# Where the output weights of a decoder step are split into high and low parts: in the stage of the chunk rows, or beside the last group of products

## The chip, the cores and the metric

The kernel runs on one core of a Trainium2 chip. The metric is the device time of one execution in microseconds (us). A core has five engines, each with an in-order queue of its own: TensorE (PE) for matrix products, VectorE (DVE), ScalarE (ACT), GpSimd (POOL) and SyncE (SP), which here issues most of the DMA transfers. On-chip memory is SBUF; products are summed up in PSUM banks, from which DVE or ACT must evict them before the bank is used again. An engine waits for another by semaphores.

## What is computed

One step of a hybrid decoder layer over 1024 prompt rows and 8 × 8 sample rows (T = 1088 columns, as most tensors are held transposed), with model width D = 1024:

```
proj = h @ w_in                                  # one projection into all branches
P = (pool_mix(u_pool) * silu(z_pool)) @ w_pool_out
S = gated_rmsnorm(SSD(conv(xBC)) + D*x, z_ssm) @ w_ssm_out      # 2048 -> 1024
m = sigmoid(g_pool) * P + sigmoid(g_ssm) * S
x = x + gate * (m @ w_o)                         # w_o: 1024 x 1024
y = rmsnorm(x)
```

Products are made to fp32 precision out of a faster format, fp32r: a factor is split into a high part (a copy in fp32r) and a low part (the factor less its high part), and a product is three matmuls, high·high, high·low and low·high. So each weight has to be split once, by a copy on ACT and a subtraction on POOL or DVE, before PE can use it. This study is on the weight w_o, 4 MB, which is used only at the end.

## The kernel before, in words

The work goes through four stages.

1. **Projections** and convolution, to about 830 us. Beside them the weights w_pool_out and w_ssm_out are split (`splits`), and their halves are stored in DRAM (`wp_d`, `ws_d`).

2. **Chunk rows**, about 830 to 1130 us (L1783 to L1822). The SSD recurrence runs over 4 groups of 8 chunks, 32 steps of `seq`. For each chunk there are a load of decay terms (tile `dec` from DRAM `acs_d`, 512 KB), an exponential on ACT (L1498), DVE's L1520 and L1522, and PE's transposes and products (L1506, L1508, L1213, L1530); ACT also evicts L1511, L1513. Between them stand pieces of the dense products (`pieces`, matmuls at L359 to L361): P for all eight row blocks (`P_unit`) and S for groups 0 to 2 (`S_unit`, whose first group is evicted by ACT at L1739). PE's order of work in this stage is written down by the program (`in_line`), so PE stands wherever the next item isn't ready. From chunk 13 on, two calls per chunk go to the generator `wo_splits` (L1764 to L1781), which cuts w_o into 16 pieces of 128x512. For each piece there are a load on SP's queue into `pw` (L1771; two buffers), a copy to fp32r on ACT into `ph` (L1777; one buffer), a store of the high half from ACT's queue (L1778), a subtraction on POOL (L1779), and a store of the low half on SP's queue (L1773). The halves go to DRAM, `wo_d`.

3. **Tail**, about 1130 to 1200 us (L1829 to L1932). First the norm's scales: sums of squares (matmul, L1843), a square root on ACT (L1845), a reciprocal, eight diagonal matrices on DVE (L1851) and products that spread them (L1852) into three PSUM banks. Then come eight units, one for each block of 128 channels of m: the last group's product `S_unit(3, m)`, three blocks of 12 matmuls in three rotating PSUM banks. `m_done` (L1887 on) loads `R` from `gs_d` (the gate, 128x1088) and multiplies it by the scales on DVE (three L1891, which read PSUM), loads P's part from `m1_d`, and for each block evicts PSUM on DVE (L1898). Behind the last block stand a multiplication on DVE (L1903) and an addition on POOL (L1904), both 128x1088 with all operands in SBUF. `m_split` (L1868 on) splits the result: 64 sample columns (ACT L1871, DVE L1872) and 1024 prompt columns (ACT L1882, DVE L1883). `wo_prep(k)` loads both halves of row block k of w_o from `wo_d` (L1864, L1865; 512 KB each): blocks 0 to 3 into a tile that was freed by the earlier stage (`Y4(hp)`), block 4 into buffers of the tail, 5 to 7 only behind the last unit into tiles freed by it (`late`). `samples[k]` is the sample rows' product with block k (four matmuls, L1877). The order of instructions within an engine is set by the framework's scheduler, apart from the places where the program gives a priority or writes the order down. Weights for the products are loaded two units ahead (`ready`, L459 and L460).

4. **End**, about 1200 to 1296 us (L1978 to L2019): eight row tiles, each 8 × 3 matmuls for each half of the columns (L1995 to L1997) of m with w_o, then gate, residual and norm; a tile's output is stored while the next one is being made.

Of the kernel before, what the change touches and what calls it, by code (L numbers as in the profile page):

```python
# [8 lines left out]
F32 = mybir.dt.float32  # L9
F32R = mybir.dt.float32r  # L10
AF = mybir.ActivationFunctionType
ALU = mybir.AluOpType
# [8 lines left out]
P = 128  # L21
D = 1024
# [24 lines left out]
def tile_pool_ssd_step(  # L47
# [6 lines left out]
    nc = tc.nc  # L54
    uid = [0]

    def nm(s):
        uid[0] += 1
        return f"{s}_{uid[0]}"
# [10 lines left out]
    def open_(name, bufs, side="left"):  # L70
        cm = tc.tile_pool(name=name, bufs=bufs, side=side, reuse_waits="tile")
        kept.append(cm)
        return cm.__enter__()
# [36 lines left out]
    load = nc.sync.dma_start  # L110
    store_ = nc.scalar.dma_start
    mm = nc.tensor.matmul
    act = nc.scalar.activation
    V = nc.vector
# [224 lines left out]
    def in_line(engines, begin=False):  # L339
        traced = nc.cur_bb.bb.instructions  # L340
        for i in traced[len(traced) if begin else line[0]:]:
            if i.engine in engines:
                if i.engine in line[1]:
                    tc.add_manual_dep(i, line[1][i.engine], mybir.DependencyInfo(
                        mybir.DependencyClass.NoSync, mybir.DependencyReason.DATA), reason="in_line")
                line[1][i.engine] = i.name
        line[0] = len(traced)
# [42 lines left out]
    def dram(name, shape, dt=F32):  # L390
        return dr.tile(list(shape), dt, tag=name, name=name)
# [13 lines left out]
    def behind(engine, n=0):  # L405

        of = (i for i in reversed(nc.cur_bb.bb.instructions) if i.engine == engine)
        for _ in range(n):
            next(of)
        return tc.issue_after(next(of))  # L410
# [1070 lines left out]
    def sample_end(g):  # L1481
        sz = ckt([P, 4, P], "sz", 3)[:, :, :NS]
        load(sz, z_d[g][:, :, SEQ:])
        v = ckt([P, 4, P], "v")[:, :, :NS]
        load(v, ys_d[g])
        finish(g, SEQ, NS, v, sz)
# [219 lines left out]
    ck = right.__enter__()  # L1706
# [20 lines left out]
    def S_unit(g, m, done):  # L1727
        def run(w):
            rh = [yh[g][:, q] for q in range(4)]
            rl = [yl[g][:, q] for q in range(4)]  # L1730
            yield from gemm_(w, rh, rl, 4, done(m))
        return (ready(ws_d[g][m]), run)
# [22 lines left out]
    def pieces():  # L1755
        ws = first_ws
        nxt = len(ws)
        for i, (pf, run) in enumerate(prods):
            while nxt < len(prods) and nxt <= i + 1:
                ws[nxt] = prods[nxt][0]()  # L1760
                nxt += 1
            yield from run(ws.pop(i))
    pc_ = pieces()
    wo_d = [dram(f"wo{k}", [P, 2, D]) for k in range(8)]  # L1764

    def wo_splits():
        raws = {}
        for n in range(18):
            if n < 16:
                raws[n] = ck.tile([P, 512], F32, tag="pw", name=nm("pw"), bufs=2)  # L1770
                load(raws[n], w_o[0, n // 2 * P:n // 2 * P + P, n % 2 * 512:n % 2 * 512 + 512])  # L1771
            if n > 1:
                load(wo_d[(n - 2) // 2][:, 1, n % 2 * 512:n % 2 * 512 + 512], raws.pop(n - 2))  # L1773
            yield
            if n < 16:
                hi = ck.tile([P, 512], F32R, tag="ph", name=nm("ph"), bufs=1)
                act(hi, raws[n], AF.Copy)  # L1777
                store_(wo_d[n // 2][:, 0, n % 2 * 512:n % 2 * 512 + 512], hi.bitcast(F32))  # L1778
                nc.gpsimd.tensor_tensor(raws[n].bitcast(F32R), raws[n], hi.bitcast(F32), ALU.subtract)  # L1779
            yield  # L1780
    wos = wo_splits()  # L1781
    RATE = 2.56
    FRONT = 4  # L1783

    def products(t):

        nonlocal made
        while made < RATE * t:
            next(pc_, None)
            made += 1  # L1790
# [5 lines left out]
        next(pc_)  # L1796
    next(seq[0])
    for i in range(len(seq)):
        if i > 12:
            next(wos, None)  # L1800
        if i + 1 < len(seq):
            with behind(mybir.EngineType.DVE, 1 - i) if i < 2 else ExitStack():
                next(seq[i + 1])
        products(i + 0.4)
        if i > 0:
            next(seq[i - 1], None)
        if i > 12:
            next(wos, None)
        next(seq[i], None)
        if i % NC == 3:  # L1810
            sample_end(i // NC)
        if i + 3 < len(seq):
            next(seq[i + 3])
        if i + 2 < len(seq):
            with behind(mybir.EngineType.Activation) if i == 0 else ExitStack():
                next(seq[i + 2])
        products(i + 1.0)
    next(seq[-1], None)
    for it in (pc_, wos):
        for _ in it:  # L1820
            pass
    in_line((mybir.EngineType.PE,))  # L1822
    right.__exit__(None, None, None)
    while right_all:
# [3 lines left out]

    mp = ctx.enter_context(tc.tile_pool(name="mp", bufs=8, side="right", reuse_waits="tile"))  # L1829
    mq = open_("mq", 5)  # L1830

    def M(shape=(P, T), dt=F32):
        return mq.tile(list(shape), dt, tag="m", name=nm("m"))
# [7 lines left out]
    for c in range(9):  # L1841
        n = min(P, T - c * P)
# [5 lines left out]
    for c in range(9):  # L1848
        n = min(P, T - c * P)
# [4 lines left out]
    wo, mh, ml = [None] * 8, [None] * 8, [None] * 8  # L1854
    w4 = [Y4(hp), Y4(hp)]
    pso = [PB(), PC()]
    samples = []

    def wo_prep(k, mem):
        if k < 4:  # L1860
            hi, lo = w4[0][:, k, :D], w4[1][:, k, :D]
        else:
            hi, lo = mem((P, D), F32R), mem((P, D), F32R)
        load(hi.bitcast(F32), wo_d[k][:, 0])  # L1864
        load(lo.bitcast(F32), wo_d[k][:, 1])  # L1865
        wo[k] = (hi, lo)

    def m_split(k, mem):  # L1868

        sh = sm.tile([P, P], F32R, tag="stc", name=nm("sh"), bufs=4)  # L1870
        act(sh[:, 0:NS], acc[k][:, SEQ:], AF.Copy)  # L1871
        V.tensor_tensor(sh[:, NS:P], acc[k][:, SEQ:], sh[:, 0:NS].bitcast(F32), ALU.subtract)  # L1872

        def sample_mm():
            for part in wo[k]:
                for half in range(2):
                    mm(pso[half], sh, part[:, half * 512:half * 512 + 512],  # L1877
                       start=(k == 0 and part is wo[k][0]), stop=(k == 7 and part is wo[k][1]))
        samples.append(sample_mm)
        hi, lo = mem((P, SEQ), F32R), mem((P, SEQ), F32R)  # L1880
        for o, n in (((0, 384), (384, 384), (768, 256)) if k == 7 else ((0, SEQ),)):
            act(hi[:, o:o + n], acc[k][:, o:o + n], AF.Copy)  # L1882
            V.tensor_tensor(lo[:, o:o + n], acc[k][:, o:o + n], hi[:, o:o + n].bitcast(F32), ALU.subtract)  # L1883
        mh[k], ml[k] = hi, lo
# [22 lines left out]
    def tail_unit(m):  # L1907
        pf, run_ = S_unit(3, m, m_done)

        def run(w):  # L1910
            for _ in run_(w):
                pass
            if m < 5:
                wo_prep(m, M)
            if m < 7:
                m_split(m, M8 if m < 4 else G)
            if m < 5:
                with tc.high_priority(PRIO):
                    samples[m]()
        return (pf, run)  # L1920
    run_units([tail_unit(m) for m in range(8)])
    y4 = [Y4(hs), Y4(hs)]
# [4 lines left out]
    for k in (5, 6):  # L1927
        wo_prep(k, late)
        samples[k]()
    wo_prep(7, late)  # L1930
    m_split(7, late)
    sample_mm = samples[7]  # L1932
# [116 lines left out]
```

## Time and profile before

| what | value |
|---|---|
| median of three runs | 1296.04 us (1295.9, 1296.04, 1298.21) |
| the profiled execution's own time | 1297.28 us |
| its span on the core | 1295.4 us (1.88 us lie around it) |
| mean granted clock of PE | 0.996 |
| PE busy in the span | 1258.9 us, 97% |
| DVE, ACT, POOL busy | 893.3, 699.5, 671.9 us |
| moved by DMA | 251.68 MB, 194 GB/s in the mean |

How to read the rows of the profile. A row of a timeline is: start in us, length in us, engine, line of the program, operation, output tile <- input tiles, shape and type of output and inputs, and how many such instructions the row takes together (x3 is three behind each other). Brackets at the end tell how long the engine stood idle before it, and what ended the idle time: "[2.96 <-DMA pw<-in_w_o]" is 2.96 us, ended by the landing of the transfer from w_o into `pw`. Matmuls overlap in the records, so that successive starts, not lengths, give PE's pace. A queue's rows (SPq) are the issue of a transfer and not its duration. A row of groups gives the count of one kind of instruction, then smallest, median and largest duration in ns, and when the first and the last began.

### The profile page before, as it was taken

To read this page: it belongs to the slowest core of one execution; us is meant where nothing else is said; L and a number is where in the kernel's file an instruction comes from. 1 tells how busy PE (TensorE), PEld (TensorE's weight loads), DVE (VectorE), ACT (ScalarE), POOL (GpSimd) and SP (SyncE) were. 2 spreads that over 40 slices of the span, in tenths; PEclk is the share of its full clock that TensorE was granted. 3 is DMA by queue.
4 is the path that set the end of the run, shared out by engine and by line. 5 is a ranking of instruction groups with operands and counts; after the bars stand their busy time and mean duration, and the time that the engine had idled before them with its cause. 6 is when DMAs were issued, how large, how long until landed. Compare 5 with 4: busy or idle time off the path is not lost.

```text
span 1295.4 us, 26382 instructions
## 1 busy us (share of the span) xinstructions
PE 1258.9 (97%) x9739; PEld 1170.7 (90%) x9739; DVE 893.3 (69%) x1512; ACT 699.5 (54%) x1658; POOL 671.9 (52%) x563
## 2 busy tenths in 40 slices
PE   7999999999999999999999999999998999999998
PEld 6779999989999999999999999888897889999786
DVE  4686678966979688676766675577665877476433
ACT  4665347365656555555666543687886776201111
POOL 1007668677868777564445444266675656214000
PEclk9999999999999999999999999999999999999999
DMA  9736355465456544444566574999887665475631
GB/s 330 242 115 223 113 163 164 147 203 177 136 161 212 157 144 149 151 146 135 169 182 192 154 207 159 336 362 382 296 270 249 200 210 171 160 262 161 227 105 50
DMA packets 233793, 251.68 MB, mean 194 GB/s; under 512 B 31265, under 2 KB 177905, under 8 KB 233658
## 3 DMA queue, kind: packets, MB, share of 16 engines
q1 hardware_dynamic: 161568, 171.60, 41.6%
q10 hardware_dynamic: 72098, 78.41, 17.6%
q8 instruction: 77, 1.26, 0.4%
q14 instruction: 50, 0.41, 0.1%
HBM read 167.06 MB, written 83.01 MB: 193 GB/s over the span
## 4 chain that ended last, share of the span: by engine, by line
PE 73%; issue 8%; DMA 6%; POOL 4%; ACT 4%; DVE 4%; ACTq 0%; SPq 0%; POOLq 0%; DVEq 0%
PE mm L608 7%; PE ps L608 7%; PE ps L609 7%; PE ps L610 7%; PE mm L610 6%; PE mm L609 6%; PE mm L359 4%; PE mm L360 4%; PE mm L361 4%; PE ps L1213 2%; PE ps L1997 2%; PE ps L1995 2%; PE ps L1996 2%; PE pc L1530 2%; PE ps L1216 2%
## 5 line engine op out<-in xcount | busy, mean ns | idle before, releaser
L168 POOL TENSOR_TENSOR wlo<-rawA,whi 128x512 fp32r<-128x512 f32 x120 | 180.0, 1505 | 176.8 <-ACT whi L165 100.3
L168 POOL TENSOR_TENSOR wlo<-raw,whi 128x512 fp32r<-128x512 f32 x92 | 147.2, 1607 | 123.2 <-ACT whi L165 109.3
L359 PE MATMUL mm<-Y,whi 128*128 128x352 f32 (+1 forms) x480 | 164.2, 342 | 2.0 <-ACT G L1739 1.4
L360 PE MATMUL mm<-Y,whi 128*128 128x352 f32 (+1 forms) x480 | 158.1, 329 | 1.0 <-DVE Y L1566 1.0
L361 PE MATMUL mm<-Y,wlo 128*128 128x352 f32 (+1 forms) x480 | 157.5, 328 | 0.0
L608 PE MATMUL mm<-Y,whi 128*128 128x272 f32 x496 | 146.5, 295 | 0.7 <-DVE GA L624 0.5
L610 PE MATMUL mm<-Y,wlo 128*128 128x272 f32 x496 | 144.2, 291 | 2.9 <-POOL wlo L168 2.4
L608 PE MATMUL ps<-Y,whi 128*128 128x272 f32 x496 | 143.4, 289 | 2.3 <-ACT o L808 2.2
L609 PE MATMUL ps<-Y,whi 128*128 128x272 f32 x496 | 143.0, 288 | 0.0
L609 PE MATMUL mm<-Y,whi 128*128 128x272 f32 x496 | 142.6, 288 | 0.0
L610 PE MATMUL ps<-Y,wlo 128*128 128x272 f32 x496 | 142.6, 287 | 0.0
L1056 DVE SCALAR_TENSOR_TENSOR GA<-GA,cvT,GA 128x1112 f32<-128x1112 f32 x72 | 128.5, 1787 | 1.6 <-ACT GA L1053 1.5
L165 ACT ACTIVATE whi<-rawA 128x512 fp32r<-128x512 f32 x125 | 78.3, 627 | 88.8 <-PE ps L609 44.9
L165 ACT ACTIVATE whi<-raw 128x512 fp32r<-128x512 f32 x96 | 58.9, 627 | 105.7 <-DVE raw L554 51.3
L359 PEld LDWEIGHTS mm<-Y,whi 128*128 128x128 f32 x480 | 90.8, 189 | 8.8 <-issue 4.6
L610 PEld LDWEIGHTS mm<-Y,wlo 128*128 128x128 f32 x496 | 93.4, 188 | 4.7 <-POOL wlo L168 3.5
L608 PEld LDWEIGHTS mm<-Y,whi 128*128 128x128 f32 x496 | 93.3, 188 | 3.4 <-ACT whi L165 0.7
L608 PEld LDWEIGHTS ps<-Y,whi 128*128 128x128 f32 x496 | 93.3, 188 | 2.9 <-ACT o L808 2.4
L609 PEld LDWEIGHTS mm<-Y,whi 128*128 128x128 f32 x496 | 93.4, 188 | 0.9
L610 PEld LDWEIGHTS ps<-Y,wlo 128*128 128x128 f32 x496 | 93.4, 188 | 0.0
L609 PEld LDWEIGHTS ps<-Y,whi 128*128 128x128 f32 x496 | 93.3, 188 | 0.0
L360 PEld LDWEIGHTS mm<-Y,whi 128*128 128x128 f32 x480 | 90.8, 189 | 1.7 <-DVE Y L1566 1.6
(450 smaller groups left out, 3801.1 us busy)
## 6 DMA issues: line engine op xcount, KB each, us to landing
rawA<-in_w_in SPq DMA_DIRECT2D x46, 512.0 KB
dec<-acs_d SPq DMA_DIRECT2D x32, 512.0 KB
xbc<-GA ACTq DMA_DIRECT2D x24, 512.0 KB
xb<-xbc SPq DMA_DIRECT2D x32, 384.0 KB
rawA<-in_w_in SPq DMA_DIRECT2D x32, 256.0 KB
pw<-in_w_ssm_out ACTq DMA_DIRECT2D x32, 256.0 KB
ws<-ph ACTq DMA_DIRECT2D x32, 256.0 KB
ws<-pw SPq DMA_DIRECT2D x32, 256.0 KB
```

What stands on the lines that cost most here:

```text
L165: ins = act(hi[:, :, :ncols], raw[:, :, :ncols], AF.Copy)
L168: (eng or nc.gpsimd).tensor_tensor(lo[:, :, :ncols], raw[:, :, :ncols], hi[:, :, :ncols].bitcast(F32), ALU.subtract)
L359: mm(ps[:, :n], a, rh[k][:, o:o + n], start=(k == 0), stop=False)
L360: mm(ps[:, :n], a, rl[k][:, o:o + n], start=False, stop=False)
L361: mm(ps[:, :n], b, rh[k][:, o:o + n], start=False, stop=(k == nk - 1))
L608: mm(p, hi, ah, start=(k == 0), stop=False)
L609: mm(p, hi, al, start=False, stop=False)
L610: mm(p, lo, ah, start=False, stop=(k == 3))
L1056: V.scalar_tensor_tensor(d[:, :n], rp[:, k:k + n], cvT[:, 24 * k + mc:24 * k + mc + 1], d[:, :n], ALU.mult, ALU.add)
L1213: mm(o[hh], xd[:S, 2 * q + hh, :], dec[:S, 2 * q + hh], start=True, stop=state is None)
L1216: mm(o[hh], state[:, h * 64:h * 64 + 64], cE[:, h], start=False, stop=True)
L1530: mm(pu, bt, xw.rearrange("p h d -> p (h d)"), start=True, stop=True)
```

## The change

`wo_splits` and its calls in the chunk rows' loop go. The first five row blocks (`LATE = 5`) are loaded from w_o as they are in `wo_prep`, 512 KB each into a new pool `mr` (tag `wr`, two buffers), copied to fp32r by ACT and subtracted by POOL, and both parts stay on chip. The last three are split by a new function `wo_store`, called behind units 2, 3 and 4: load, ACT copy into `wh` (one buffer), store of the high half, subtraction on DVE, store of the low half, both stores issued by SP. Behind the last unit `wo_prep` loads them from DRAM as before. The sample rows' products follow one unit later than before (`samples[m - 1]`). Two lines fewer stand ahead of the tail's functions, so that line L1898 of before, for one, is L1894 of the changed kernel (L1903: L1899; L1904: L1900; L1872: L1868; L1883: L1879; L1995: L1993).

```diff
-    wo_d = [dram(f"wo{k}", [P, 2, D]) for k in range(8)]
-
-    def wo_splits():
-        raws = {}
-        for n in range(18):
-            if n < 16:
-                raws[n] = ck.tile([P, 512], F32, tag="pw", name=nm("pw"), bufs=2)
-                load(raws[n], w_o[0, n // 2 * P:n // 2 * P + P, n % 2 * 512:n % 2 * 512 + 512])
-            if n > 1:
-                load(wo_d[(n - 2) // 2][:, 1, n % 2 * 512:n % 2 * 512 + 512], raws.pop(n - 2))
-            yield
-            if n < 16:
-                hi = ck.tile([P, 512], F32R, tag="ph", name=nm("ph"), bufs=1)
-                act(hi, raws[n], AF.Copy)
-                store_(wo_d[n // 2][:, 0, n % 2 * 512:n % 2 * 512 + 512], hi.bitcast(F32))
-                nc.gpsimd.tensor_tensor(raws[n].bitcast(F32R), raws[n], hi.bitcast(F32), ALU.subtract)
-            yield
-    wos = wo_splits()
+
+    LATE = 5
+    wo_d = {k: dram(f"wo{k}", [P, 2, D]) for k in range(LATE, 8)}
...
     for i in range(len(seq)):
-        if i > 12:
-            next(wos, None)
         if i + 1 < len(seq):
...
-        if i > 12:
-            next(wos, None)
         next(seq[i], None)
...
     mq = open_("mq", 5)
+    mr = open_("mr", 2)
...
-        load(hi.bitcast(F32), wo_d[k][:, 0])
-        load(lo.bitcast(F32), wo_d[k][:, 1])
+        if k < LATE:
+            raw = mr.tile([P, D], F32, tag="wr", name=nm("wr"))
+            load(raw, w_o[0, k * P:k * P + P, :])
+            act(hi, raw, AF.Copy)
+            nc.gpsimd.tensor_tensor(lo, raw, hi.bitcast(F32), ALU.subtract)
+        else:
+            load(hi.bitcast(F32), wo_d[k][:, 0])
+            load(lo.bitcast(F32), wo_d[k][:, 1])
         wo[k] = (hi, lo)
+
+    def wo_store(k):
+        raw = mr.tile([P, D], F32, tag="wr", name=nm("wr"))
+        load(raw, w_o[0, k * P:k * P + P, :])
+        hi = mr.tile([P, D], F32R, tag="wh", name=nm("wh"), bufs=1)
+        act(hi, raw, AF.Copy)
+        load(wo_d[k][:, 0], hi.bitcast(F32))
+        V.tensor_tensor(raw.bitcast(F32R), raw, hi.bitcast(F32), ALU.subtract)
+        load(wo_d[k][:, 1], raw)
...
-            if m < 5:
+            if m < LATE:
                 wo_prep(m, M)
             if m < 7:
                 m_split(m, M8 if m < 4 else G)
-            if m < 5:
+            if 1 < m < 5:
+                wo_store(m + 3)
+            if 0 < m <= LATE:
                 with tc.high_priority(PRIO):
-                    samples[m]()
+                    samples[m - 1]()
```

(`load` issues a transfer on SP's queue, in either direction; `store_` one on ACT's.)

More of the change, by code (lines that the diff above doesn't have):

```diff
@@ L1818, in tile_pool_ssd_step @@
     next(seq[-1], None)
-    for it in (pc_, wos):
-        for _ in it:
-            pass
+    for _ in pc_:
+        pass
     in_line((mybir.EngineType.PE,))
```

## The prediction

> **What bounds the kernel now.** I read the page's busy shares first, then the windows by stage, then each engine's timeline where TensorE (PE) stood still.
>
> ```profile
> PE 1258.9 (97%) x9739; PEld 1170.7 (90%) x9739; DVE 893.3 (69%) x1512; ACT 699.5 (54%) x1658; POOL 671.9 (52%) x563
> ```
> ```profile
> 830.00:950.00 120.00, 118.37 (x950) 104.81 (x950) 87.16 (x116) 97.16 (x271) 79.50 (x87) 1.00 0.98 336
> 950.00:1005.00 55.00, 49.81 (x392) 44.05 (x389) 32.29 (x42) 37.68 (x102) 33.02 (x36) 1.00 0.80 254
> 1005.00:1130.00 125.00, 125.00 (x987) 112.57 (x987) 88.85 (x129) 76.91 (x213) 69.41 (x88) 1.00 0.58 185
> 1130.00:1145.00 15.00, 15.00 (x92) 14.97 (x90) 5.42 (x17) 0.41 (x2) 0.00 (x0) 0.89 0.71 248
> 1145.00:1200.00 55.00, 54.41 (x312) 51.45 (x311) 42.30 (x69) 8.97 (x15) 21.05 (x9) 1.00 0.57 192
> ```
>
> PE is 97% busy: only its idle time and its own work can move the end. The windows' columns are the length, the busy time (and instructions) of PE, PEld, DVE, ACT and POOL, then the granted clock, DMA share and GB/s. The splits of w_o run from 837.8 to 992.7 us; the chunk rows go on without them to 1130. With splits PE idles 120 − 118.37 = 1.63 and 55 − 49.81 = 5.19 us; without them, 0.00. In the tail (last group of products, 1130 to 1200) it idles 0.59.
>
> **The change part by part.**
>
> *Taken out of the chunk rows.* The 5.19 us are three waits of PE, 1.42 + 2.09 + 1.68:
>
> ```profile
> 975.61 0.63 ACT L1777 ACTIVATE ph<-pw 128x512 fp32r<-128x512 f32 x1 [2.96 <-DMA pw<-in_w_o]
> 978.37 0.44 ACT L1739 ACTIVATE G<-mm 128x352 f32<-128x352 f32 x1
> 991.97 0.63 ACT L1777 ACTIVATE ph<-pw 128x512 fp32r<-128x512 f32 x1 [4.82 <-DMA wo<-ph]
> 1003.60 1.06 ACT L1498 ACTIVATE cE<-dec 128x1024 f32<-128x1024 f32 x1 [3.34 <-DMA dec<-acs_d]
> ```
> ```profile
> 980.54 1.22 DVE L1520 TENSOR_TENSOR dec<-dec,ps 128x1024 f32<-128x1024 f32 x1 [7.26 <-POOL sz L1475]
> 1000.34 1.22 DVE L1520 TENSOR_TENSOR dec<-dec,ps 128x1024 f32<-128x1024 f32 x1 [6.18 <-ACT ps L1513]
> ```
> ```profile
> 978.86 0.43 PE L359 MATMUL mm<-Y,whi 128*128 128x352 f32 x1 [1.42 <-ACT G L1739]
> 983.15 0.63 PE L1506 MATMUL ps<-ident,xb 128*128 128x128 f32 x4 [2.09 <-DVE cE L1522]
> 1002.84 0.30 PE L1508 MATMUL ps<-ident,xb 128*128 128x128 f32 x1 [1.68 <-DVE cE L1522]
> ```
>
> ACT stood 2.96 us before the copy at 975.61, for its load, and 4.82 us before the one at 991.97, because `ph` has one buffer whose store had not landed. ACT works in order, so the eviction L1739 (978.37), then L1513, came late; DVE L1520 stood 7.26 and 6.18 us; PE came last. All three waits hang on ACT standing for a split. The stage also loses 16 copies, 16 subtractions, 48 transfers of 256 KB (12 MB; SP issues 32, ACT 16):
>
> ```profile
> L1777 ACT ACTIVATE ph<-pw x16: 612/619/632, 837.8 to 992.0; 128x512 fp32r<-128x512 f32 x16
> L1779 POOL TENSOR_TENSOR pw<-pw,ph x16: 1273/1296/1457, 839.0 to 992.7; 128x512 fp32r<-128x512 f32 x16
> ```
>
> That is 16 × 0.619 = 9.9 us of ACT, 16 × 1.296 = 20.7 of POOL, none itself on PE's path. Order of PE's instructions in the stage is unchanged. What would be late next is the load of `dec` (ACT's 3.34 us at 1003.60), in a stage with 12 MB less to move. Bounds: 0 (that load takes over) to 5.19 + 1.63 = 6.8. I take **−5.2**, as the 125 us without splits show no wait.
>
> *Put beside the last group.* Rows 0–4: a 512 KB load, an ACT copy, a POOL subtraction each. Rows 5–7: load, copy, store, DVE subtraction, store, and both halves loaded later. DMA falls from 12 + 8 MB to 10, but all in the tail and the stretch behind it; SP issues there go from 16 to 20. ACT gains eight copies of 128x1024 (1.04 each, row below), 8.3 us, and it is busy 0.41 of 15 and 8.97 of 55: hidden. DVE gains 3 × 1.21 (at 42.30 of 55); POOL 5 × 2.4 = 12 us (2.54 × 1024/1088, from L1904), on top of 21.05 of 55. Mean load is no bound; order is, and who blocks whom:
>
> ```profile
> 1151.40 1.29 DVE L1903 TENSOR_TENSOR G<-G,R 128x1088 f32<-128x1088 f32 x1
> 1153.61 2.85 DVE L1903 TENSOR_TENSOR G<-G,R 128x1088 f32<-128x1088 f32 x1
> 1156.85 2.30 DVE L1872 TENSOR_TENSOR sh<-G,sh 128x64 fp32r<-128x64 f32 x1
> 1160.84 1.21 DVE L1883 TENSOR_TENSOR m<-G,m 128x1024 fp32r<-128x1024 f32 x1
> 1161.97 0.22 DVE L1872 TENSOR_TENSOR sh<-G,sh 128x64 fp32r<-128x64 f32 x1
> ```
> ```profile
> 1152.77 2.54 POOL L1904 TENSOR_TENSOR G<-G,m 128x1088 f32<-128x1088 f32 x1 [34.67 <-DVE G L1903]
> 1156.54 2.53 POOL L1904 TENSOR_TENSOR G<-G,m 128x1088 f32<-128x1088 f32 x1 [1.23 <-DVE G L1903]
> ```
>
> The same L1903 takes 1.29 alone and 2.85 when it starts inside POOL's addition of 1152.77–1155.31; L1872 takes 0.22 alone and 2.30 inside 1156.54–1159.07, ending with it. So a DVE instruction with both inputs in SBUF and a POOL one shut each other out. Each new subtraction on POOL is therefore 2.4 us in which DVE's in-order queue can stand, with PE's evictions (L1898) behind it.
>
> The Trainium skill, "SBUF — State Buffer", section "🔬 SBUF: two separate sides", says that the two engines' shared port pair is an exclusive lock, kept for the whole instruction by whoever starts first. It speaks against this change, and the two rows above agree with it; by plain sharing of the bandwidth the tail's term below would be about 0.
>
> ```profile
> 1135.02 2.05 PE L1843 MATMUL ps<-ones,sq_acc 128*128 128x1 f32 x18
> ```
> ```profile
> 1155.51 1.04 ACT L1882 ACTIVATE m<-G 128x1024 fp32r<-128x1024 f32 x1
> ```
>
> The chain, in the times of before. The earliest POOL can start row 0 is about 1136 (the products of group 2 end where the sums of squares begin, 1135.0, with rows 0 and 1 taken to be loaded already; a copy of this shape takes 1.04); rows 0 and 1 end about 1141. Row 2's load takes the buffer freed at 1138.6. A 544 KB load took 1166.31 to 1169.99 = 3.7 us, so it lands about 1142.4 and is subtracted until 1145.8; row 3's load then follows and its subtraction runs about 1151.6–1154.0. There it meets the chain of L1903 and L1904. Alternating from there (multiply 1.29, addition 2.5): first multiply ends 1155.3, addition 1157.9, second pair 1161.8, DVE's subtraction of row 6 1162.9, POOL's row 4 until 1165.5, DVE's L1883 1166.6, the third multiply 1167.8 and the third addition 1170.4; before, the third multiply ended 1166.28.
>
> ```profile
> 1164.99 1.29 DVE L1903 TENSOR_TENSOR G<-G,R 128x1088 f32<-128x1088 f32 x1
> 1166.20 1.42 DVE L1898 TENSOR_TENSOR G<-mm,G 128x384 f32<-128x384 f32 x3
> 1169.99 1.42 DVE L1891 TENSOR_TENSOR R<-ps,R 128x512 f32<-128x512 f32 x3 [2.37 <-DMA R<-gs]
> ```
> ```profile
> 1145.51 0.32 SPq L459 DMA_DIRECT2D whi<-ws  x1
> ...
> 1166.31 0.32 SPq L1888 DMA_DIRECT2D R<-gs  x1
> ```
> ```profile
> 1166.80 0.44 PE L359 MATMUL mm<-Y,whi 128*128 128x384 f32 x1
> 1168.99 0.32 PE L359 MATMUL mm<-Y,whi 128*128 128x352 f32 x1
> 1174.40 0.44 PE L359 MATMUL mm<-Y,whi 128*128 128x384 f32 x1 [0.48 <-DVE G L1898]
> ```
>
> DVE's order changes at this place: before, the third multiply is followed by all three evictions of group 3 (1166.20, 1.42). After, behind the first eviction stand L1872 of the second unit (shut out until 1170.4), three L1891 (1.42) and L1883 (1.21); the other evictions end about 1173.5. PE's second block of the next product wants that bank and began at 1168.99: it starts about 1173.6, **+4.6**, from which before's wait of 0.48 at 1174.40 is taken, as it falls inside: **+4.1**. Bounds: 0 (the subtractions fall between evictions) to 6 (a second such meeting, 2.5 − 0.6).
>
> Other queues. SP now has stores behind ACT and DVE, and ahead of weight loads; the weights issued at 1145.51 are used at 1166.80, 21 us later, so a hold of some 4 us is covered, and if it were not, PE would stand for those 4 us once. The square root's table load and scales now stand behind two row copies:
>
> ```profile
> 1116.59 1.28 ACT L1845 ACT_TABLE_LOAD   x1 [0.46 <-ACT xD L1550]
> 1137.11 0.41 ACT L1845 ACTIVATE rs<-ps,eps 128x8 f32<-128x8 f32 x2 [19.23 <-PE ps L1843]
> 1142.83 1.05 PE L1852 MATMUL ps<-dg,ones 128*128 128x128 f32 x8
> ```
>
> The scales come about 1138.3 instead of 1137.1, and PE asks for them at 1142.83: cost 0, up to 1.3 + 1.04 if two more copies go ahead.
>
> *The end.* Before, two sample products wait for their rows:
>
> ```profile
> 1205.23 0.47 PE L1877 MATMUL ps<-Y,sh 128*128 128x512 f32 x1 [0.38 <-DMA Y<-wo]
> 1206.89 0.50 PE L1877 MATMUL ps<-Y,sh 128*128 128x512 f32 x1 [0.27 <-DMA Y<-wo]
> ```
>
> With samples one unit later, more of PE's work stands between these loads and their use: **−0.65**, between 0 and −0.65. Rows 5–7 are stored some 25 us before they are read.
>
> Sum: −5.2 + 4.1 − 0.65 = −1.75. The profiled execution has 1297.28 us (span 1295.4 and 1.88 around it), 1.24 above the median of 1296.04: 1295.5 in its terms, **1294.3** against the median.
>
> **The rivals.**
>
> *The meeting on DVE misses PE.* If row 3's load lands some 4 us sooner, or DVE's queue leaves evictions ahead of the shut-out L1872, POOL's subtractions fall in its idle time (34.67 us before 1152.77). For it: 21.05 of 55 busy. Against it: only two raw buffers, so row 3 waits for row 1. Tail 0 to 1.3: 1296.04 − 5.85 = 1290.2 to 1291.5.
>
> *Another wait takes the place of the splits' (slower).* ACT at L1498 waits for `dec`, whose load is on the chain of waits for
>
> ```profile
> 813.58 8.80 DMA dec<-acs_d
> ```
>
> 8.80 us at its longest there, and 3.34 at 1003.60, after the last split. If those loads hold PE at 978, 983 and 1002 as well, the stage gains under 0.8, and the tail's +4.1 decides: 1296.04 − 0.5 + 4.1 − 0.65 = 1299.0 (1298.6 to 1300.1). It decides from a gain below 0.8. For it: DMA 0.98 busy from 830 to 950. Against: 12 of the stage's megabytes go, and the waits are charged to transfers of the splits.
>
> *The clock.* In 1130–1145 the granted clock is 0.89, which costs 15 × 0.11 = 1.65 us. If PE's stand of 4 us sets off another such stretch, 1294.3 + 1.65 = 1296.0. For it: the row itself; against: 5.19 us of idle time in 950–1005 left the clock at 1.00. The Trainium skill, "TensorE: Matmul & The Clock Gate", section "Why this matters", warns of PE-idle gaps above about 3 us; no run here shows such a gap in the tail.
>
> **How the numbers follow.** Forecast 0.45 (its own range 1292.5 to 1296.8: gain 6.2 to 3.7, tail 3.3 to 4.6), meeting missed 0.27, other wait 0.18, clock 0.10. A measurement of this kernel tells about 0.2%, 2.6 us, from no change: faster is below 1293.4, slower above 1298.6. Faster: 0.27 and a quarter of the forecast, 0.39. Slower: 0.17 of the second rival. The rest, 0.44, is the same. The range reaches from the first rival with the stage's whole 6.8 at half weight (1290.2 − 0.8) to the second with no gain at all and nothing at the end (1300.1): 1289.4 to 1300.2.
>
> **What would show it.** Right: no PE wait at L359, L1506 and L1508 between 970 and 1005, no DVE L1520 standing over 6 us; in the tail, DVE instructions with two SBUF inputs of 2 us and more, ending with a POOL subtraction, and one PE wait of 2 to 5 us for L1898's successor in the units 3 to 5 of the last group. Wrong: a tail without such a wait (first rival); ACT's L1498 standing for `dec` with PE behind it (second); a clock below 0.95 in the 55 us after 1145 (third); or a PE wait for `whi`, which would mean that SP's queue, not DVE's, decides.

## The result: slower, by a new wait of TensorE that the old order of the queues had hidden

| | median us | runs | against the runs of before beside it |
|---|---|---|---|
| before | 1295.97 (1292.31 to 1298.21) | 6 | |
| changed | 1303.04 (1299.62 to 1304.68) | 6 | 1.0056, 95% interval 1.0037 to 1.0074 |

The prediction was 1294.3, no change that can be told, with 0.17 for slower; the result lies above its range. The profiled execution took 1303.4 us (span 1301.7, mean granted clock 0.992), against 1297.28 (1295.4, 0.996) before.

The page of the changed kernel gives PE's busy time:

```profile
PE 1261.2 (97%) x9739; PEld 1173.0 (90%) x9739; DVE 906.2 (70%) x1515; ACT 700.9 (54%) x1650; POOL 661.0 (51%) x552
```

Before, 1295.4 − 1258.9 = 36.5 us of the span were idle; now it is 1301.7 − 1261.2 = 40.5. So of the 6.3 us, 4.0 are idle time and 2.3 are the same 9739 matmuls taking longer. The windows of the changed kernel (length, then busy time of PE, PEld, DVE, ACT, POOL, granted clock, DMA share, GB/s) tell where:

```profile
830.00:950.00 120.00, 111.17 (x869) 97.72 (x869) 79.03 (x109) 82.79 (x237) 54.96 (x63) 0.97 0.78 253
950.00:1005.00 55.00, 55.00 (x444) 49.06 (x441) 36.67 (x48) 43.02 (x120) 34.48 (x43) 1.00 0.69 203
1005.00:1130.00 125.00, 125.00 (x989) 112.55 (x988) 89.88 (x128) 77.00 (x213) 70.22 (x88) 1.00 0.58 182
...
1145.00:1200.00 55.00, 51.00 (x296) 48.16 (x295) 53.04 (x75) 13.61 (x18) 26.83 (x11) 1.00 0.73 250
```

In 950 to 1005 the 5.19 us of idle time are gone, as forecast (55.00 of 55.00). But in 830 to 950, where before idled 1.63, PE now idles 8.83, and the clock, 1.00 before, is 0.97. In the tail idle time goes from 0.59 to 4.00, which was forecast too. PE's waits from 830 to 1130, and then those from 1125 to 1215 (what waits, for whom; total, count, longest):

```profile
PE ps L1508 <- DVE cE L1522: 5.3, 1, 5.3
PE pc L1530 <- ACT bt L1511: 1.1, 1, 1.1
PE ps L1213 <- DVE dec L1520: 1.1, 1, 1.1
PE mm L360 <- POOL Y L1479: 1.1, 1, 1.1
```
```profile
PE mm L359 <- DVE G L1894: 2.5, 2, 1.3
PE ps L1873 <- DVE sh L1868: 1.5, 2, 1.1
```

One wait of 5.3 us is new. It stands where the first chunk group hands over to the second, and the chain behind it is read from ACT's timeline, then DVE's and PE's:

```profile
900.29 1.06 ACT L1498 ACTIVATE cE<-dec 128x1024 f32<-128x1024 f32 x1 [4.10 <-DMA dec<-acs_d]
...
913.40 0.58 ACT L1550 ACTIVATE xD<-ps 128x512 f32<-128x512 f32 x1
914.00 0.40 ACTq L1551 DMA_DIRECT2D out<-xD  x1
...
921.46 1.28 ACT L1525 ACTIVATE xD<-xb,Dv 128x128 f32<-128x128 f32 x4 [5.46 <-DMA out<-xD]
...
923.31 0.28 ACT L1513 ACTIVATE ps<-xb 128x128 f32<-128x128 f32 x1
```
```profile
923.68 1.22 DVE L1520 TENSOR_TENSOR dec<-dec,ps 128x1024 f32<-128x1024 f32 x1 [9.62 <-ACT ps L1513]
```
```profile
926.17 0.45 PE L1508 MATMUL ps<-ident,xb 128*128 128x128 f32 x1 [5.27 <-DVE cE L1522]
```

At the end of a group ACT copies the final state (L1550, `fo`) into one of the two buffers of the tile `xD`, and a transfer stores it (issued at 914.00). The next L1525 waits until that store has landed, 7.5 us after its issue; that the two share a buffer is what e3 tests below. ACT works in order: L1513 comes only at 923.31, DVE's L1520, idle for 9.62 us, starts behind it, and PE stands 5.27 us. Before, the same pair stood on ACT's queue with other work between them:

```profile
909.14 0.57 ACT L1550 ACTIVATE xD<-ps 128x512 f32<-128x512 f32 x1
909.75 0.40 ACTq L1551 DMA_DIRECT2D out<-xD  x1
...
914.22 0.62 ACT L1777 ACTIVATE ph<-pw 128x512 fp32r<-128x512 f32 x1
...
918.52 1.27 ACT L1525 ACTIVATE xD<-xb,Dv 128x128 f32<-128x128 f32 x4
```

The store was issued 4.25 us sooner, and L1525 came 8.8 us behind it: no wait. PE's order in this stage is the same in both kernels, but the scheduler, with the splits gone, put the instructions of ACT, DVE, POOL and SP into another order: between the state's store and L1525 stand only three instructions (1.5 us, from 914.50 to 916.00); L1513, which DVE waits for, stands behind this L1525 (923.31 and 921.46), where before it came first (914.74 and 918.52); and L1498 (900.29, after 4.10 us for its load) comes ahead of an earlier L1525 (904.91) that before came first (898.32 and 902.65). I had compared PE's order only.

The wait itself could be read from the kernel before. ACT's timeline shows it, shorter, at two later handovers; behind the second, in the 125 us without splits, PE has no wait:

```profile
993.00 1.28 ACT L1525 ACTIVATE xD<-xb,Dv 128x128 f32<-128x128 f32 x4 [0.40 <-DMA out<-xD]
...
1057.70 1.28 ACT L1525 ACTIVATE xD<-xb,Dv 128x128 f32<-128x128 f32 x4 [1.03 <-DMA out<-xD]
```

In the changed kernel these two are 1.73 and 2.51 us (992.29 and 1062.03), still without a wait of PE; only the one of 5.46 us reaches it.

Behind the gap PE ran at half speed for some 4 us. Two successive matmuls of 128x384 in that stretch, and two of the same shape later (start, length):

```profile
929.09 0.52 PE L360 MATMUL mm<-Y,whi 128*128 128x384 f32 x1
929.41 0.52 PE L361 MATMUL mm<-Y,wlo 128*128 128x384 f32 x1
...
1141.40 0.34 PE L361 MATMUL mm<-Y,wlo 128*128 128x384 f32 x1
1141.58 0.34 PE L359 MATMUL mm<-Y,whi 128*128 128x384 f32 x1
```

The step is 0.32 instead of 0.18 us. From 926.2 to 930.5 that costs about 2 us, which is most of the 2.3 that the matmuls lost.

### The profile page after: what moved, and what is told of

Same layout as the page of the kernel before. It is cut to its first block, busy times and chain, and to the rows that moved or that the text cites. A ratio compares the mean times of both kernels' runs of the same rounds, so it can differ in the third digit from the quotient of the medians.

```text
span 1301.7 us, 26273 instructions
## 1 busy us (share of the span) xinstructions
PE 1261.2 (97%) x9739; PEld 1173.0 (90%) x9739; DVE 906.2 (70%) x1515; ACT 700.9 (54%) x1650; POOL 661.0 (51%) x552
## 4 chain that ended last, share of the span: by engine, by line
PE 74%; DMA 6%; issue 6%; DVE 5%; POOL 4%; ACT 3%; ACTq 0%; SPq 0%; POOLq 0%; DVEq 0%
PE ps L608 6%; PE ps L609 6%; PE mm L608 6%; PE ps L610 6%; PE mm L610 6%; PE mm L609 6%; PE mm L359 5%; PE mm L360 4%; PE mm L361 4%; PE ps L1213 2%; PE ps L1993 2%; PE ps L1995 2%; PE ps L1994 2%; POOL wlo L168 2%; DMA dec<-acs_d 2%
```

## The experiments

Each was timed in 12 runs beside runs of the kernel before on the same chip; ratios are to those.

| experiment | chunk rows | tail | median us | before beside it | ratio, 95% interval |
|---|---|---|---|---|---|
| e1 | as before | as changed | 1298.74 | 1295.88 | 1.0018, 1.0004 to 1.0032 |
| e2 | as changed | as before | 1299.48 | 1295.88 | 1.0029, 1.0018 to 1.0040 |
| e3 | changed, own buffer for the state | as changed | 1293.87 | 1295.88 | 0.9982, 0.9972 to 0.9992 |
| e4 | as changed | row subtractions on DVE | 1299.12 | 1295.88 | 1.0024, 1.0013 to 1.0035 |
| e5 | as e3 | as e4 | 1292.23 | 1295.21 | 0.9980, 0.9967 to 0.9992 |
| e6 | as e3 | sample products two units late | 1294.97 | 1295.21 | 0.9995, 0.9982 to 1.0008 |
| e7 | as e3 | as before | 1292.14 | 1295.21 | 0.9976, 0.9962 to 0.9990 |
| e8 | as e3 | e4 and e6 | 1291.43 | 1295.21 | 0.9973, 0.9961 to 0.9985 |
| e9 | as e3 | e8, stored rows on POOL | 1296.87 | 1294.71 | 1.0018, 1.0002 to 1.0033 |
| e12 | as e3 | e8, no stored rows | 1291.29 | 1294.71 | 0.9974, 0.9964 to 0.9985 |

My theory was that the loss comes from the chunk rows, by the new order of the queues, the wait for the state's store and the half clock behind it; the rival, that it comes from the tail, as a cost that I had sized too small.

### e1 and e2: one stage of each kernel

e1 adds to the changed kernel the 16 splits in the chunk rows, with their old calls and a scratch tensor that nothing reads:

```diff
+    wox = [dram(f"wox{k}", [P, 2, D]) for k in range(8)]
+    wos = wo_splits()
...
+        if i > 12:
+            next(wos, None)
```

> The changed kernel with the 16 splits also left in the chunk rows, stored to scratch that nobody reads; the tail is the changed one. The queues of ACT, SP, DVE and POOL in the chunk rows stand in the order of the kernel before. Theory A (the loss comes from the chunk rows: without the splits the scheduler ordered ACT's and SP's queues anew, and one PE wait of 5.27 us with a half clock behind it resulted): that wait is absent, PE idles about 6.8 us between 830 and 1130 as before, and the tail alone costs about +2.8 us (+3.4 tail, -0.65 end), so about 1298.8 against 1296.0. Rival B (the loss comes from the tail, through DMA or POOL): the time stays at that of the changed kernel or above, 1303 or more.

e2 takes the splits out of the kernel before and puts nothing in their place:

```diff
-    wos = wo_splits()
...
-        load(hi.bitcast(F32), wo_d[k][:, 0])
-        load(lo.bitcast(F32), wo_d[k][:, 1])
+        load(hi.bitcast(F32), ws_d[0][k].rearrange("p a k c -> p (a k c)"))
+        load(lo.bitcast(F32), ws_d[1][k].rearrange("p a k c -> p (a k c)"))
```

> The kernel before with the 16 splits taken out of the chunk rows and nothing put in their place; the tail loads, with transfers of the same size, parts of another split weight in place of the halves of w_o, so the last product is not that with w_o. The order of the queues in the chunk rows is that of the changed kernel, the tail that of before. Theory A: the chunk rows lose as in the changed kernel (PE idle 8.8 instead of 6.8 us, and some 2 us of half clock), so about 1300 although 16 copies, 16 subtractions and 12 MB are gone. Rival B: the stage gains its 5 us, about 1291.

e2 computes something else at the end: its tail loads parts of another weight in the place of w_o's halves. Measured were 1298.74 and 1299.48. Theirs are +2.9 and +3.6 us over before; together 6.5 of the changed kernel's 7.1. So the loss has two parts of about the same size, and within their intervals (0.5 to 4.1 and 2.3 to 5.2 us) they add up. In e1 the long wait is absent, and PE's waits of the kernel before are back (830 to 1240; L1917, L1896 and L1891 are L1894, L1873 and L1868 of the changed kernel):

```profile
PE ps L1508 <- DVE cE L1522: 2.7, 1, 2.7
PE mm L359 <- DVE G L1917: 2.5, 2, 1.3
PE ps L1506 <- DVE cE L1522: 2.1, 1, 2.1
PE mm L359 <- ACT G L1739: 1.6, 1, 1.6
PE ps L1896 <- DVE sh L1891: 1.5, 2, 1.1
```

In e2, with 12 MB, 16 copies and 16 subtractions fewer than before and the tail of before, ACT stands again for the state's store, and PE behind it. The first row is ACT's timeline, the second PE's:

```profile
920.00 1.27 ACT L1525 ACTIVATE xD<-xb,Dv 128x128 f32<-128x128 f32 x4 [5.00 <-DMA out<-xD]
```
```profile
924.71 0.45 PE L1508 MATMUL ps<-ident,xb 128*128 128x128 f32 x1 [4.82 <-DVE cE L1522]
```

Taking work away, alone, made the kernel slower.

### e3 and e7: a buffer of its own for the state

```diff
-            fo = ckt([P, 4, P], "xD")
+            fo = cl.tile([P, 4, P], F32, tag="fo", name=nm("fo"), bufs=1)
```

> The changed kernel with one edit: the tile in which a group's final state is stored has a buffer of its own instead of one of the two of the tile xD. Theory A1 (the 5.27 us of PE come from ACT standing 5.46 us for the landing of that store before it may write xD): the wait and the half clock behind it go, about 7.3 us: 1295.7. Rival A2 (the store is only the last of several late things at this place; the loads of dec or xb come just as late): PE still waits 3 us or more near 920, 1300 or more.

> The kernel without the splits in the chunk rows (the tail is that of before and loads parts of another split weight in place of the halves of w_o, so the last product is not that with w_o), with the buffer of its own for the stored state. This is the chunk rows' term alone, without the new wait. Theory A1 (taking the splits out is worth the 5.2 us that the prediction gave it, if ACT doesn't stand for the state's store): PE idles about 1.7 us between 830 and 1130 instead of 6.8, and the time is about 1296 - 5.1 = 1290.8. Rival A3 (part of the gain of this edit in the changed kernel came from its tail): 1293 or more.

One line takes 9.2 us off the changed kernel (1303.04 to 1293.87) and makes it faster than before; e7, which is e2 with this line, has 1292.14 instead of 1299.48. The windows over 830 to 1130, of e3 and then of e7:

```profile
830.00:1130.00 300.00, 298.30 (x2358) 266.64 (x2357) 208.75 (x288) 203.18 (x569) 158.30 (x195) 1.00 0.69 219
```
```profile
830.00:1130.00 300.00, 297.07 (x2345) 265.33 (x2344) 207.43 (x287) 203.41 (x568) 159.51 (x194) 1.00 0.68 216
```

PE idles 1.70 and 2.93 us there, against 6.82 before and 8.83 in the changed kernel, at a clock of 1.00. The edit changes the order of ACT and SP once more, but it is the buffer that counts: L1525 now comes 0.3 us behind the store's issue (911.21 and 910.89) and doesn't wait for it. In e3 ACT still stands 3.06 us for a load of `dec` ahead of this place (897.34 in its timeline), and PE doesn't feel it: the wait for the store decides. e7 gained 3.1 us on before, where I had expected 5.1. That is the chunk rows' term without the new wait, and its interval (1.3 to 4.9 us) leaves out 5.2.

### e4: the row blocks' subtractions on DVE

```diff
-            nc.gpsimd.tensor_tensor(lo, raw, hi.bitcast(F32), ALU.subtract)
+            V.tensor_tensor(lo, raw, hi.bitcast(F32), ALU.subtract)
```

> The changed kernel with the subtractions of row blocks 0 to 4 on DVE (5 of about 1.2 us) instead of POOL (5 of 2.4). Theory C (the tail's 4 us of PE idle come from DVE being shut out by POOL's subtractions, its evictions queued behind): PE's idle time between 1160 and 1180 falls from 4.0 to about 1.5, so about 1300.5 against 1303; DVE's diagonal scalings take 0.22 us each again instead of 0.66 and more. Rival D (DVE is simply short of time there): idle 4 us or more, 1303 or more.

In the changed kernel DVE's timeline in the tail is full of stretched instructions; POOL's follows it:

```profile
1142.86 2.66 DVE L1832 TENSOR_SCALAR dg<-ident,rs 128x128 f32<-128x128 f32 x4
...
1158.53 2.96 DVE L1899 TENSOR_TENSOR G<-G,R 128x1088 f32<-128x1088 f32 x1
...
1164.91 2.54 DVE L1868 TENSOR_TENSOR sh<-G,sh 128x64 fp32r<-128x64 f32 x1
```
```profile
1140.14 4.71 POOL L1849 TENSOR_TENSOR Y<-wr,Y 128x1024 fp32r<-128x1024 f32 x2 [18.10 <-ACT Y L1848]
...
1157.94 2.40 POOL L1849 TENSOR_TENSOR Y<-wr,Y 128x1024 fp32r<-128x1024 f32 x1 [8.16 <-ACT Y L1848]
1160.30 7.06 POOL L1900 TENSOR_TENSOR G<-G,m 128x1088 f32<-128x1088 f32 x2
```

L1899 started inside POOL's subtraction of 1157.94 and ended 1.15 us behind it, 1.29 being its own time before: it had waited for nearly all of it. e4 took 1299.12, 3.9 us less. PE's idle time from 1160 to 1180 went to 2.80 instead of the 1.5 expected: the waits for the sample columns (1.5) are gone, those for evictions (L1894) are not (2.8 instead of 2.5). Why is in e4's DVE timeline:

```profile
1143.62 0.87 DVE L1832 TENSOR_SCALAR dg<-ident,rs 128x128 f32<-128x128 f32 x4
...
1161.48 3.08 DVE L1861 TENSOR_TENSOR wr<-wr,wh 128x1024 fp32r<-128x1024 f32 x1
1164.48 0.51 DVE L1894 TENSOR_TENSOR G<-mm,G 128x352 f32<-128x352 f32 x1
1164.92 2.13 DVE L1868 TENSOR_TENSOR sh<-G,sh 128x64 fp32r<-128x64 f32 x1
```

Now it is the change's other new instruction, DVE's subtraction for the stored rows (L1861, 1.21 us alone), that is shut out by POOL's additions, with evictions behind it. These additions follow each other on POOL:

```profile
1159.96 7.00 POOL L1900 TENSOR_TENSOR G<-G,m 128x1088 f32<-128x1088 f32 x2 [37.16 <-DVE G L1899]
```

So the exclusion is shown, and my chain had put it at one instruction only. The profile accounts for 1.2 us of the 3.9; the profiled run was the slowest of its 12 (1302.25), and where the rest went isn't settled.

### e5, e6 and e8: the edits together

e5 is e3 with e4. e6 is e3 with the sample products two units behind and without priority, and e8 has all three:

```diff
-            if 0 < m <= LATE:
-                with tc.high_priority(PRIO):
-                    samples[m - 1]()
+            if 1 < m <= LATE + 1:
+                samples[m - 2]()
```

> The changed kernel with the buffer of its own for the stored state and with the subtractions of row blocks 0 to 4 on DVE. Both edits gained alone (1303.0 to 1293.9, and to 1299.1). Theory C (they act at different places): PE idle between 830 and 1130 about 1.7 us, the tail's 3.6 us wait for the sample columns shorter than 1.5, about 1290.5. Rival D (DVE is short of time in the tail once PE comes to it sooner): 1293 or more.

> The changed kernel with the buffer of its own for the stored state, and the sample rows' products without priority and two units behind instead of one. Theory E (the 3.62 us that PE stands at such a product, and the half clock of 2 us behind it, are there only because the product stands ahead of products that are ready): both go, about 1293.9 - 4 = 1290. Rival F (DVE is late, not the product early: PE stands as long at the next product whose PSUM bank DVE has not evicted): 1292.5 or more.

> All three edits: own buffer for the stored state, subtractions on DVE, sample products without priority and two units behind. If each wait is its own: PE idle in the tail under 1 us, about 1289.5, faster than before by 0.5%. If DVE's time is the bound of the tail: no better than the better of the two it is made of.

They took 1292.23, 1294.97 and 1291.43. e6 is a miss: with POOL's subtractions left in place, a later sample product only moves the wait. e3 had one gap of 3.62 us at such a product; behind it stands DVE's L1861 again, beside POOL's additions (PE's, DVE's and POOL's timeline of e3):

```profile
1158.22 0.80 PE L1873 MATMUL ps<-Y,sh 128*128 128x512 f32 x1 [3.62 <-DVE sh L1868]
```
```profile
1152.26 3.62 DVE L1861 TENSOR_TENSOR wr<-wr,wh 128x1024 fp32r<-128x1024 f32 x1 [2.54 <-ACT wh L1859]
```
```profile
1149.76 5.04 POOL L1900 TENSOR_TENSOR G<-G,m 128x1088 f32<-128x1088 f32 x2
```

In e6 the one gap of 3.62 us became four of 0.37 to 1.45, 4.2 us in all (2.6 for evictions, 1.5 for sample columns). e5 is between its two expectations. e8 is too by its median, but its tail idles 2.9 us where under 1 was expected, and its time can't be told from e5's, so that "no better than the better of the two" isn't ruled out. Both are faster than before, with two waits for evictions left in each, 1.29 and 1.6 us.

### e9 and e12: the rows by way of DRAM

e9 is e8 with L1861 on POOL; e12 is e8 without `wo_store`: all eight blocks are loaded, copied and subtracted on chip, the last three behind the last product. The first edit is e9's, the second a part of e12's.

```diff
-        V.tensor_tensor(raw.bitcast(F32R), raw, hi.bitcast(F32), ALU.subtract)
+        nc.gpsimd.tensor_tensor(raw.bitcast(F32R), raw, hi.bitcast(F32), ALU.subtract)
...
-            if 1 < m < 5:
-                wo_store(m + 3)
```

> The version with three edits (1291.4), and the three subtractions of row blocks 5 to 7 on POOL instead of DVE. Left over in its tail were two PE waits of 1.29 and 1.62 us for evictions, behind a subtraction of row 5 to 7 on DVE that took 3.10 instead of 1.21 us beside POOL's additions. Theory C (what is left is that shut-out): the two waits fall under 1.5 us together, about 1290. Rival G (any 2.4 us more on POOL there delay its additions and so the same chain): no gain, 1291.4 or more.

> The version with three edits, without the stores of row blocks 5 to 7: all eight are loaded, copied and subtracted (DVE) on chip, the last three behind the last product when tiles come free. 3 MB of stores, 3 MB of loads and three DVE subtractions leave the tail. Theory H (the way over DRAM costs the tail its last 2.9 us of waits): they go, and rows 5 to 7 are ready when the end asks for them: about 1288.5. Rival I (with two raw buffers the last row comes late, 3.7 us for its load, 1.0 for its copy and 1.2 for its subtraction behind a freed buffer): PE stands some 3 to 6 us near 1200, 1292 or more.

e9 lost some 5 us to e8 (ratios 1.0018 and 0.9973). POOL's subtractions beside DVE's instructions shut out others: its waits for evictions are 3.2 us and for sample columns 1.6, 1.9 more than e8's in all. Behind one of them, of 1.94 us, PE also ran at half speed from 1162.9 to 1166.1, some 1.5 us more; where the rest of the 5 went isn't settled. That is the rival's side. e12 has 1291.29, no more than e8: its waits for evictions fell from 2.9 to 1.9 us, and the feared wait for the last rows doesn't appear. So by the profiles the way by DRAM costs about a microsecond, which the times (0.9974 and 0.9973) don't show, and it isn't needed: e12 and e8 are 0.26% and 0.27% faster than before, though not told apart from e3 and e5.

## Why the prediction was wrong, point by point

- **The step that failed** is the chunk rows' −5.2: "Order of PE's instructions in the stage is unchanged. What would be late next is the load of `dec`". The three old waits did go (55.00 of 55.00 in 950 to 1005). But the other engines' orders are not unchanged, and what came late next was a store that shares a tile with the next chunk's work. With it the term is +2.0 of idle time and some 2 of half clock, and alone, in e2, +3.6 in all; without it (e7) it is −3.1, so that it was also sized too large. That the 125 us without splits show no wait of PE, my reason for the term, was true and said nothing of ACT, which stood for that store in them too (1.03 us at 1057.70).
- The second rival, another wait in place of the splits', is what happened, with a chance of 0.18 and the wrong transfer: I named the load of `dec`, which stood (4.10 us) but isn't what decides. It was priced as a gain that fails (1299.0), not as a wait larger than those removed.
- The third rival, the clock, came too, behind the 5.27 us in the chunk rows and not in the tail. I had given each rival alone, but a long enough wait brings the other with it: 1296.0 + 2.0 of idle time + 2 of half clock + 3.45 for tail and end is 1303.5, where 1303.0 was measured. That sum was made afterwards, and its last term is the forecast's.
- **The tail's +4.1 held in size**: idle time from 1160 to 1180 is 4.00 us against 0.59, so +3.4. The mechanism, POOL and DVE shutting each other out with evictions behind, held. The place didn't: instead of one wait of 4.6 there are four (1.10, 1.32, 0.39, 1.19), two of them at sample products, where none was forecast; that they add up to nearly the forecast is luck. By e4 the row subtractions on POOL carry the 1.5 at the sample products. What carries the 2.5 at the evictions isn't shown: with those subtractions on DVE they are 2.8, with DVE's new subtraction shut out by POOL's additions, and e12, without the stored rows, still has 1.9.
- **The end's −0.65 held**: no PE wait for `wo` is left; from 1200 to 1240 PE is busy 40.00 of 40.00 us, where it was 39.35. Tail and end, forecast as +3.45, are +2.9 in e1 (interval 0.5 to 4.1); its profile also has 0.8 us more idle time in the chunk rows than before (7.61 against 6.82), so they may be worth less.
- DMA and SP, costed at nothing, cost nothing that shows: no PE wait for `whi`, and e12, with 6 MB less to move, is level with e8 (ratios 0.9974 and 0.9973).
- Three slips changed nothing. The forecast's own range ends at 1296.3 by its terms (1296.04 − 3.7 + 4.6 − 0.65), not 1296.8; the overall range ends at 1300.1, as in the second rival, not 1300.2; and row 3 doesn't wait for row 1's buffer, as the first rival has it: in the changed kernel row 5's load took that one (1144.87), and row 3's went out at 1151.06, behind row 2's subtraction (1147.37 to 1149.78), as the chain has it.

## What to carry to other kernels

Where a scheduler orders the queues, taking instructions out of a stage is also a new order for what stays: compare the order on every engine, and for each in-order engine ask which of its waits had work between it and what it waits for. A tile that shares its buffers with one that is stored makes the next writer wait for that store's landing (7.5 us at the first handover here, 4.0 and 4.5 at the next two), hidden only as long as there is enough other work between. A removed wait is worth its whole length only if nothing else waits behind the same place, and a new wait can cost the clock as well, as those of 5.27, 3.62 and 2.71 us did here.

## What the runs showed of the hardware

- Small scalings stretch beside POOL as well: four TENSOR_SCALAR of 128x128 on DVE, a tensor and a column of scalars from SBUF each, took 0.88 us together before (L1851), 0.87 in e4, and 2.66 and 3.00 in the changed kernel, where POOL subtracts at that time. The Trainium skill, "SBUF — State Buffer", section "Who interferes with whom", names `tensor_scalar` among the operations that can contend; the four rows agree.
- Gaps of PE of 5.27 us (changed kernel), 3.62 (e3) and 2.71 (e1) were each followed by 3 to 6 us at half clock: granted were 0.55 from 926 to 931, 0.56 from 1160 to 1165, and 0.55 from 1003 to 1006.5. The Trainium skill, "TensorE: Matmul & The Clock Gate", section "Why this matters for your kernels", has the line at about 3 us; the first two gaps agree, and the third doesn't. Nor do these runs show a safe length below it: behind a gap of 1.94 us in e9 the clock was 0.50 from 1163 to 1166, and behind two of 1.03 and 1.05 us close together in e4 it was 0.61 from 837 to 840, while it stayed at 1.00 behind one of 2.09 us before (983 to 989) and one of 2.11 in e1 (982.6 to 991).
